# A two-layer hybrid attention block: sinks added by token, ones rows by DMA, output weights split over two steps, tail items spread over half tiles

## The chip, the cores and the metric

The kernel runs on one core of a Trainium2 chip. Its time is the device time of one execution in microseconds (us). Before the change three runs gave 1835.01 us as the median (1831.78 to 1839.63). Engines are named as the profile names them: PE (TensorE, matrix products), DVE (VectorE), ACT (ScalarE), POOL (GpSimd) and SP, which here only issues DMAs. Each engine works through its instructions in the order in which the program gives them, and waits at each for what it needs.

## The reference

Two layers (DEPTH = 2) over 1280 tokens, 256 of context and 1024 latent, at width 1024. A layer is

```
h   = adaLN-modulated RMSNorm(x)
p   = h @ w_in                                 # columns of four head groups, each with a SiLU gate
A   = multi-head latent attention, 4 heads
B   = global attention, 4 heads on 2 key heads
C   = window attention (|q - k| <= 128) + context keys, 4 heads, a sink in each softmax
D   = Mamba-2 scan, both directions
x   = x + gate * (concat(A, B, C, D) @ w_out)
```

Context tokens read only context tokens. The window heads have a sink, one learned number per head that joins each token's softmax as one more column and is then dropped, so it only adds to the softmax's denominator:

```
sink_col = jnp.broadcast_to(sink.astype(jnp.float32).reshape(kvh, g)[None, None, :, :, None, None], s_ctx.shape[:-1] + (1,))
p = jax.nn.softmax(jnp.concatenate([s_ctx, s_loc, sink_col], axis=-1), axis=-1).astype(v.dtype)
out = einsum(p over context keys, v_ctx) + einsum(p over window keys, v_band)      # the sink's column has no value
```

The second layer computes no context rows after its keys and values, and a last RMSNorm follows it.

## The kernel before

**Stages.** For each layer in turn: norm, `in_proj`, `attention`, `out_proj`. A float32 product is made of three products of rounded halves (L127 to L130: hi by hi, hi by lo, lo by hi), so each weight is fetched (`_raw`), cast to `_hi` and subtracted to `_lo`.

**Units of attention.** The pairs of heads come in the order (1,0), (1,1) for B, (0,0), (0,1) for A, (2,0), (2,1) for C. The tokens form `GROUPS = [(0,256), (256,512), (768,512)]`; a pair goes through them in the order 1, 2, 0 in the first layer and 1, 2 in the second. One (pair, group) is a unit, `main` at L1199. It goes over key blocks of 128. In each, PE makes scores (L1223, L1225, L1226), ACT takes the exponential into a tile `P` (L1227), values are multiplied in batches (L1235), and `add` sums the `P`s over the blocks: the first two in one POOL instruction (L1244, it creates `ac`), then block by block, on DVE for head 0 of every second block and on POOL else (L1250).

**The maximum.** Scores are shifted by each token's maximum, which `maxima` finds ahead, spread by `plan` over the unit before: PE `ps_s` (L1143, L1145) into a ring of three PSUM tiles, DVE reductions `mp` (L1147), at the end `mt` (L1166; for C also L1169, the maximum with the sink). Then `row` transposes `mt` (L1173), ACT negates it to `ng` (L1175), and SP writes `ng` into row 64 (or 96) of the second query tile `ql` (L1177). The matching row of the key tile holds ones (L1043, DVE copies), so the product L1226 subtracts the maximum.

**The sink.** After the second block of a C unit, `sink` (L1252) makes on ACT exp(sink - maximum) from that row of `ql`, one partition by up to 512 tokens, per head (L1256), and DVE adds it into partition 64 of `ac` (L1258).

**The tail.** What ends a unit runs in pieces during the next: `output` (L1282 ACT, L1283 POOL), two empty pieces, `token_sums` (PE transposes `ac` into `ps_sum` L1293, ACT sums over keys with 16 short instructions `junk` L1296, DVE reciprocal `asum` L1299), an empty piece, `finish` (PE `ps_rt` L1303, ACT `rrow` L1305, DMAs through DRAM into `rb`, DVE `y` L1313).

**Output weights.** During the units of the last pair, (2,1), up to three pieces of `w_out` each are fetched and split (`late`, L1543: SP DMA L1550, DVE cast L1557, DVE subtraction L1558, in halves of 512 columns). The landing tile `wo_raw` comes from the same ring of six tiles (`bg`) as `P`. What is then missing of the eight pieces is fetched and split at the start of `out_proj` (L286 SP, L289 ACT, L290 DVE). `out_proj` makes two halves of 24 products per token tile (L128 to L130, `ps_o`), casts and splits `y` (`yh` L1388 on ACT, `yl` L1389 on DVE), and runs every tail item that is left after its first tile (L1437).

**What sets the order.** In attention PE's order is written out by hand (`order_of_pe`); the other engines' order is made by the framework's scheduler.

Of the kernel before, what the change touches and what calls it, by code (L numbers as in the profile page):

```python
# [17 lines left out]
P = 128  # L18
# [39 lines left out]
def hybrid_block(ctx, tc, x, ctxt, c_t, w_fm, w_tm, w_mod, b_gate, p_col, p_row, w_qu, w_kvu, w_out,  # L58
# [125 lines left out]
    d_rms = [dp.tile([NTILE, P], F32, name=f"d_rms{i}") for i in range(3)]  # L184
    n_rms = [0]
    d_x = dp.tile([NT, DM], F32, name="d_x")

    pcol, prow, modt = {}, {}, {}

# [846 lines left out]
    def attention(L, res, need_ctx, y, late, ahead):  # L1036
# [2 lines left out]
        groups = GROUPS if need_ctx else GROUPS[1:]  # L1039

        def ones_row(tok, row):
            for lo, n in ((0, NCTX), (NCTX, NLAT)):
                nc.vector.tensor_copy(tok(lo, n, row, row + 1), ones[row:row + 1, 0:1].to_broadcast([1, n]))  # L1043

        def rows(tok, p0, src, with_ctx=True):

# [80 lines left out]
        def maxima(op, gi):  # L1127
            lo, n = GROUPS[gi]
            nt = n // P
            br, kd = op["br"], op["kd"]  # L1130
            km = kd if br == 0 else P
            npc = 1 if gi == 0 else (3 if br < 2 else 2)
            st = {}

            def scored(h, parts, dst):

                qh = op["q"][h][0]
                kh = op["k"][h][0] if br == 0 else op["k"][0][0]
                p = ps("MX", name="ps_s")
                w = parts[0][2]  # L1140
                for u, (t, k0, w, mo) in enumerate(parts):
                    o = p[:, u * w:(u + 1) * w]
                    mm(o, lhsT=qh(lo + t * P, P, 0, km), rhs=kh(k0, w, 0, km), start=True, stop=mo is None)  # L1143
                    if mo is not None:
                        mm(o, lhsT=ident_r, rhs=mask_r[:, mo:mo + w], start=False, stop=True)  # L1145
                nu = len(parts)
                nc.vector.tensor_reduce(out=dst, in_=p[:, :nu * w].rearrange("p (u k) -> p u k", u=nu), axis=AX.X, op=ALU.max)  # L1147

            def begin():
                st["mp"] = small([P, 2, 4, 3], "mp", "mp", 2)  # L1150

            def ctx_part(h, t2):
                scored(h, [(t2 + u, 0, NCTX, None) for u in range(2)], st["mp"][:, h, t2:t2 + 2, 0])

            def lat_part(h, t, c):
                if br < 2:
                    scored(h, [(t, NCTX + c * 512, 512, None)], st["mp"][:, h, t, 1 + c:2 + c])
                else:
                    i = lo // P + t
                    j0, j1 = max(2, i - 1), min(NTILE - 1, i + 1)  # L1160
                    scored(h, [(t, j0 * P, (j1 - j0 + 1) * P, (j0 - i + 1) * P)], st["mp"][:, h, t, 1:2])

            def end():
                mt = st["mt"] = small([P, 8], "mt", "mt", 2)
                mv = mt[:, 0:2 * nt].rearrange("p (h t) -> p h t", h=2)
                nc.vector.tensor_reduce(out=mv, in_=st["mp"][:, :, 0:nt, 0:npc], axis=AX.X, op=ALU.max)  # L1166
                if br == 2:
                    p0 = op["pair"] * 2
                    nc.vector.tensor_tensor(out=mv, in0=mv, in1=sink8[:, p0:p0 + 2].unsqueeze(2).to_broadcast([P, 2, nt]), op=ALU.max)  # L1169

            def row():
                pm = ps("TR", name="ps_m")
                nc.tensor.transpose(pm[0:2 * nt, 0:P], st["mt"][:, :2 * nt], ident)  # L1173
                ng = tm((8, P), F32R, name="ng")
                nc.scalar.activation(out=ng[0:2 * nt, :], in_=pm[0:2 * nt, 0:P], func=AF.Copy, scale=-1.0)  # L1175
                for h in range(2):
                    nc.sync.dma_start(out=f32(op["q"][h][1](lo, n, kd, kd + 1)), in_=f32(ng[h * nt:(h + 1) * nt, :]))  # L1177

            r = [begin]
            for h in range(2):  # L1180
                r += [lambda h=h, t=t: ctx_part(h, t) for t in range(0, nt, 2)]
                if gi > 0:
                    r += [lambda h=h, t=t, c=c: lat_part(h, t, c) for t in range(nt) for c in range(2 if br < 2 else 1)]
            return r + [end], row
# [14 lines left out]
        def main(op, gi, steps, tail):  # L1199
# [38 lines left out]
            def add(bi, pts):  # L1238
# [7 lines left out]
                else:  # L1246
                    s = sums[0]
                    for h in range(2):
                        eng = nc.vector if h == 0 and bi % 2 == 0 else nc.gpsimd
                        eng.tensor_tensor(out=s[:, h, c0:c0 + w], in0=s[:, h, c0:c0 + w], in1=pts[:, h, :w], op=ALU.add)  # L1250

            def sink():  # L1252
                for h in range(2):
                    hd = op["pair"] * 2 + h
                    es = tm(name="es")
                    nc.scalar.activation(out=es[64:65, :n], in_=f32(op["q"][h][1](lo, n, 64, 65)), func=AF.Exp,  # L1256
                                         scale=HEAD_SCALE, bias=pr[64:65, PR_SINK + hd:PR_SINK + hd + 1])
                    nc.vector.tensor_tensor(out=sums[0][64:65, h, :n], in0=sums[0][64:65, h, :n], in1=es[64:65, :n], op=ALU.add)  # L1258

            nb = -(-len(blocks) // BATCH)  # L1260
            ends = [-(-len(blocks) * (b + 1) // nb) - 1 for b in range(nb)]
# [28 lines left out]
            def token_sums(h):  # L1290
                pss = ps("TR", name="ps_sum")
                for t in range(nt):
                    nc.tensor.transpose(pss[:, t * P:(t + 1) * P], sums[0][:, h, t * P:(t + 1) * P], ident)  # L1293
                for t in range(nt):
                    junk = tm((P, P), name="junk")
                    nc.scalar.activation(out=junk, in_=pss[:, t * P:(t + 1) * P], func=AF.Copy, scale=2.0,  # L1296
                                         accum_out=ss[:, h * nt + t:h * nt + t + 1])
                if h == 1:
                    nc.vector.reciprocal(out=ss[:, :2 * nt], in_=ss[:, :2 * nt])  # L1299

            def finish():
# [9 lines left out]
                    nc.sync.dma_start(out=rb[h * 64:h * 64 + 64, :n],  # L1311
                                      in_=dr[h * nt:(h + 1) * nt, :].rearrange("t q -> (t q)").unsqueeze(0).to_broadcast([64, n]))
                nc.vector.tensor_tensor(out=y[br * 2 + op["pair"]](lo, n), in0=rb[:, :n], in1=o[:, :n], op=ALU.mult)  # L1313
            idle = lambda: None
            return tail + [output, idle, idle, lambda: [token_sums(h) for h in range(2)], idle, finish]

        def plan(blocks, pieces, row, loose):

# [23 lines left out]
            return r + more, row  # L1342

        first, row = prep(*pairs[0])
        yield first + [row]
        y_slots, tail = [], []
        order_of_pe = ExitStack()
        order_of_pe.enter_context(tc.manual_schedule(engines={mybir.EngineType.PE}))
        for i, (br, pair) in enumerate(pairs):
            op = ops[br, pair]  # L1350
            if need_ctx and i == 0:
                pk = Slot([P, 4, NCTX], F32, "y_cx")
                y_slots.append(pk)
            if need_ctx and br == 2:
                pk = res["ssd"].y_slots[0]
            s = Slot([P, NLAT], F32, f"y{br}{pair}")
            y_slots.append(s)
            y[br * 2 + pair] = Tok(pk.t[:, br * 2 + pair - (2 if br == 2 else 0), :] if need_ctx else None, s.t)
            for gi in gorder:
                pieces, row, loose = [], None, []  # L1360
                if gi == 1:
                    pieces, row = maxima(op, 2)
                    if need_ctx:
                        loose, late_row = maxima(op, 0)
                elif gi == 2:
                    if i + 1 < len(pairs):
                        pieces, row = prep(*pairs[i + 1])
                if i + 1 == len(pairs):
                    loose = loose + sum((late() for _ in range(N_LATE)), [])
                if i + 1 == len(pairs) and gi == 0:  # L1370
                    ahead()
                steps = plan(len(key_blocks(br, gi)), pieces, row, loose)
                if gi == 2 and need_ctx:
                    steps[4][0].append(late_row)
                tail = main(op, gi, steps, tail)
        order_of_pe.close()
        while len(tail) > 5:
            tail.pop(0)()
        if not need_ctx:
            ahead()  # L1380
        yield y_slots, tail
# [10 lines left out]
    def out_proj(L, y, need_ctx, wo, tail, y_slots, pairs):  # L1392
# [27 lines left out]
        for t in ts:  # L1420
# [5 lines left out]
            for j in range(2):  # L1426
# [7 lines left out]
                if j == 0:  # L1434
                    ssq = small([P, 2], "ssq", "ssq", 4)
                half_ssq(xt.t, j, ssq)
            if t == ts[0]:  # L1437
                for f in tail:
                    f()
            if not last:  # L1440
                if t >= 2:
                    nc.sync.dma_start(out=d_x[c, :], in_=xt.t)
# [73 lines left out]
    for L in range(DEPTH):  # L1516
# [23 lines left out]
        def ahead():  # L1540
            y_pairs[2] = y_pair(y, 2)

        def late():  # L1543

            st = []

            def first():
                if len(wo) < 8 and len(free_slots) >= 2:
                    raw = bg(name="wo_raw")
                    nc.sync.dma_start(out=raw, in_=w_out[L, len(wo)])  # L1550
                    st.extend([raw, Slot([P, 1024], F32R, "wo_hi"), Slot([P, 1024], F32R, "wo_lo")])
                    wo.append(st[1:])

            def half(j):
                if st:
                    js = slice(j * 512, (j + 1) * 512)
                    nc.vector.tensor_copy(st[1].t[:, js], st[0][:, js])  # L1557
                    nc.vector.tensor_tensor(out=st[2].t[:, js], in0=st[0][:, js], in1=f32(st[1].t[:, js]), op=ALU.subtract)  # L1558
            return [first, lambda: None, lambda: half(0), lambda: half(1)]
# [95 lines left out]
```

## Time and profile before

| | us |
|---|---|
| median of three runs | 1835.01 |
| profiled execution | 1834.35 |
| its span | 1832.6 |
| PE busy | 1724.8 (94%) |
| DVE busy | 1159.6 (63%) |
| POOL busy | 777.4 (42%) |
| ACT busy | 747.1 (41%) |

The mean granted clock of PE over the span is 0.982 of full speed. Window attention (pairs of C) is at 790 to 870 us in the first layer and 1655 to 1732 in the second, each followed by its `out_proj`. A row of a timeline gives start, duration, engine, line, operation, out<-in, shape and, in brackets, how long the engine was idle before it and what ended the wait. Consecutive like instructions are put in one row with their count (x2). L12 is line 12 of the kernel before.

### The profile page before, as it was taken

Reading aid. Unit: us, or ns where it says so; the run is one execution under the profiler, and the core shown is the slowest. Engines: PE = TensorE matmul, PEld = TensorE weight load, DVE = VectorE, ACT = ScalarE, POOL = GpSimd, SP = SyncE. Lnnn points to the kernel's source line nnn. Section 1 sums busy time; section 2 is a strip of 40 time slices with the busy share of each in tenths; the row PEclk is TensorE's granted clock in tenths of the full one; section 3 lists DMA queues with packets and bytes.
Section 4 is the critical chain, followed back from the end, with each engine's and each line's share of the span. In section 5 each row is a group of like instructions: output and inputs, shape, how many; then the busy total and the mean of one; then the engine's idle time right before and its main releaser. Section 6 shows DMA issues by size and latency. Waiting matters only on the chain. (4 is left out here: it accounts for less than half of the span.)

```text
span 1832.6 us, 27875 instructions
## 1 busy us (share of the span) xinstructions
PE 1724.8 (94%) x9658; PEld 1340.1 (73%) x9658; DVE 1159.6 (63%) x2290; ACT 747.1 (41%) x2060; POOL 777.4 (42%) x735
## 2 busy tenths in 40 slices
PE   6999999999989999998999989999998999999898
PEld 4667888889975566665787768888997656667576
DVE  6867864374468766557646777753743887655753
ACT  5433433332225545455423323343322355456531
POOL 2322552132317766655324224531332477665422
PEclk9999999999999999998999989999999999999899
DMA  9474323255576232223411524231668633220511
GB/s 314 143 235 142 125 90 121 82 195 178 187 209 151 71 102 65 70 62 111 172 58 41 170 85 150 83 126 70 209 187 240 180 86 88 73 54 20 180 72 58
DMA packets 130396, 231.52 MB, mean 126 GB/s; under 512 B 13784, under 2 KB 74560, under 8 KB 130256
## 3 DMA queue, kind: packets, MB, share of 16 engines
q1 hardware_dynamic: 130256, 229.75, 40.1%
q8 instruction: 76, 1.25, 0.3%
q14 instruction: 64, 0.52, 0.1%
HBM read 161.15 MB, written 68.44 MB: 125 GB/s over the span
## 5 line engine op out<-in xcount | busy, mean ns | idle before, releaser
L1250 POOL TENSOR_TENSOR ac<-ac,P 128x512 f32<-128x512 f32 (+3 forms) x248 | 305.3, 1249 | 153.1 <-ACT P L1227 99.8
L1227 ACT ACTIVATE P<-ps_st 128x512 f32<-128x512 f32 (+3 forms) x456 | 243.2, 552 | 239.1 <-PE ps_st L1226 104.4
L1147 DVE TENSOR_REDUCE mp<-ps_s 128x1 f32<-128x512 f32 (+3 forms) x428 | 259.7, 657 | 102.0 <-PE ps_s L1143 96.3
L128 PE MATMUL ps_fm<-hh,wfm_hi 128*128 128x512 f32 x576 | 234.6, 407 | 3.3 <-DVE kb L658 1.9
L130 PE MATMUL ps_fm<-hl,wfm_hi 128*128 128x512 f32 x576 | 232.1, 403 | 1.5 <-POOL hl L403 0.7
L129 PE MATMUL ps_fm<-hh,wfm_lo 128*128 128x512 f32 x576 | 230.7, 400 | 0.0
L128 PE MATMUL ps_tm<-wtm_hi,hh 128*128 128x256 f32 x512 | 146.6, 286 | 2.0 <-DVE qkv L723 1.3
L129 PE MATMUL ps_tm<-wtm_hi,hl 128*128 128x256 f32 x512 | 145.6, 284 | 0.0
L130 PE MATMUL ps_tm<-wtm_lo,hh 128*128 128x256 f32 x512 | 145.4, 284 | 0.0
L1250 DVE TENSOR_TENSOR ac<-ac,P 128x512 f32<-128x512 f32 (+3 forms) x88 | 102.5, 1165 | 49.4 <-ACT P L1227 25.7
L130 PEld LDWEIGHTS ps_fm<-hl,wfm_hi 128*128 128x128 f32 x576 | 109.6, 190 | 27.1 <-POOL hl L403 3.2
L128 PEld LDWEIGHTS ps_fm<-hh,wfm_hi 128*128 128x128 f32 x576 | 109.9, 191 | 26.6 <-ACT hf L399 3.3
L129 PEld LDWEIGHTS ps_fm<-hh,wfm_lo 128*128 128x128 f32 x576 | 109.8, 191 | 19.4 <-issue 0.8
L1244 POOL TENSOR_TENSOR ac<-P 128x1024 f32<-128x1024 f32 (+1 forms) x30 | 66.1, 2205 | 116.2 <-ACT P L1227 103.0
L128 PE MATMUL ps_o<-wo_hi,yh 128*128 128x512 f32 x288 | 112.8, 393 | 1.4 <-ACT yh L1388 1.4
L129 PE MATMUL ps_o<-wo_hi,yl 128*128 128x512 f32 x288 | 112.8, 393 | 0.1
L130 PE MATMUL ps_o<-wo_lo,yh 128*128 128x512 f32 x288 | 112.7, 392 | 0.0
L128 PEld LDWEIGHTS ps_tm<-wtm_hi,hh 128*128 128x128 f32 x512 | 98.2, 192 | 4.3 <-issue 3.4
L130 PEld LDWEIGHTS ps_tm<-wtm_lo,hh 128*128 128x128 f32 x512 | 98.3, 192 | 0.7 <-issue 0.4
L129 PEld LDWEIGHTS ps_tm<-wtm_hi,hl 128*128 128x128 f32 x512 | 98.2, 192 | 0.5
L1235 PE MATMUL ps_acc<-P,vt 128*64 128x512 f32 (+3 forms) x416 | 84.5, 536 | 4.1 <-ACT P L1227 4.1
L1223 PE MATMUL ps_st<-qq,kk 128*128 128x512 f32 (+3 forms) x208 | 82.4, 396 | 2.9 <-DVE mp L1147 2.7
(345 smaller groups left out, 4125.0 us busy)
## 6 DMA issues: line engine op xcount, KB each, us to landing
wfm_raw<-in_w_fm_dram SPq DMA_DIRECT2D x36, 512.0 KB
wm<-in_w_mod_dram SPq DMA_DIRECT2D x64, 256.0 KB
d_q<-qkhl SPq DMA_DIRECT2D x18, 512.0 KB
wm<-in_w_mod_dram SPq DMA_DIRECT2D x16, 512.0 KB
d_gate<-th SPq DMA_DIRECT2D x32, 256.0 KB
wtm_raw<-in_w_tm_dram SPq DMA_DIRECT2D x16, 512.0 KB
qq<-d_q SPq DMA_DIRECT2D x32, 256.0 KB
wo_raw<-in_w_out_dram SPq DMA_DIRECT2D x16, 512.0 KB
```

The source lines that it names most:

```text
L128: mm(o, lhsT=lh, rhs=rh, start=first, stop=False)
L129: mm(o, lhsT=ll, rhs=rh, start=False, stop=False)
L130: return mm(o, lhsT=lh, rhs=rl, start=False, stop=last)
L1147: nc.vector.tensor_reduce(out=dst, in_=p[:, :nu * w].rearrange("p (u k) -> p u k", u=nu), axis=AX.X, op=ALU.max)
L1223: mm(st, lhsT=k(k0, 128), rhs=q(q0, 128), start=True, stop=False)
L1227: nc.scalar.activation(out=pts[:, h, :w], in_=st, func=AF.Exp, scale=op["scale"])
L1235: mm(acc[h * 64:h * 64 + 64, c0:c0 + w], lhsT=op["v"].tile(kb)[:, v0:v0 + 64], rhs=pts[:, h, :w], start=(bi == 0), stop=(bi == len(blocks) ...
L1244: nc.gpsimd.tensor_tensor(out=s[:, :, :n], in0=sums[0][:, :, :n], in1=pts[:, :, :n], op=ALU.add)
L1250: eng.tensor_tensor(out=s[:, h, c0:c0 + w], in0=s[:, h, c0:c0 + w], in1=pts[:, h, :w], op=ALU.add)
```

## The change

Five edits. (1) The ones rows of key tiles are written by DMA from a DRAM row `d_one`, which one DMA makes at the start; DVE's 32 copies go, SP gets 32 issues more. (2) The sinks are added where a token's sums stand: `end` makes the negated maximum `mr` on DVE (in all 30 units), a C unit adds the sink to it (128x8), takes the exponential on ACT (128x8) and adds it into `asum` before the reciprocal. The 20 instructions of L1256 on ACT and the 20 of L1258 on DVE go. (3) `late` may also run for the pair before the last, in groups 2 and 0, two pieces each, if three slots are free. (4) Empty tail items are dropped before `out_proj`, and one tail item runs per half tile. (5) Four empty pieces are put behind the first unit's `row`.

```diff
+    d_one = dp.tile([1, NT], F32, name="d_one")
+    nc.sync.dma_start(out=d_one.rearrange("o (a b) -> o a b", b=P), in_=ones[0:1, :].unsqueeze(1).to_broadcast([1, NTILE, P]))
...
         def ones_row(tok, row):
-            for lo, n in ((0, NCTX), (NCTX, NLAT)):
-                nc.vector.tensor_copy(tok(lo, n, row, row + 1), ones[row:row + 1, 0:1].to_broadcast([1, n]))
+            rows(tok, row, d_one)
...
             def end():
-                mt = st["mt"] = small([P, 8], "mt", "mt", 2)
+                mt = small([P, 8], "mt", "mt", 2)
...
+                st["mr"] = op["mr", gi] = small([P, 8], "mr", "mr", 4, F32R)
+                nc.vector.tensor_scalar(out=st["mr"][:, :2 * nt], in0=mt[:, :2 * nt], scalar1=-1.0, scalar2=None, op0=ALU.mult)
...
-                nc.scalar.activation(out=ng[0:2 * nt, :], in_=pm[0:2 * nt, 0:P], func=AF.Copy, scale=-1.0)
+                nc.scalar.copy(ng[0:2 * nt, :], pm[0:2 * nt, 0:P])
...
+            es = [None]
+
             def sink():
-                for h in range(2):
-                    hd = op["pair"] * 2 + h
-                    es = tm(name="es")
-                    nc.scalar.activation(out=es[64:65, :n], in_=f32(op["q"][h][1](lo, n, 64, 65)), func=AF.Exp,
-                                         scale=HEAD_SCALE, bias=pr[64:65, PR_SINK + hd:PR_SINK + hd + 1])
-                    nc.vector.tensor_tensor(out=sums[0][64:65, h, :n], in0=sums[0][64:65, h, :n], in1=es[64:65, :n], op=ALU.add)
+
+                es[0] = small([P, 8], "es", "es", 3)
+                v = es[0][:, :2 * nt].rearrange("p (h t) -> p h t", h=2)
+                p0 = op["pair"] * 2
+                nc.vector.tensor_tensor(out=v, in0=f32(op["mr", gi][:, :2 * nt]).rearrange("p (h t) -> p h t", h=2),
+                                        in1=sink8[:, p0:p0 + 2].unsqueeze(2).to_broadcast([P, 2, nt]), op=ALU.add)
+                nc.scalar.activation(out=es[0][:, :2 * nt], in_=es[0][:, :2 * nt], func=AF.Exp, scale=HEAD_SCALE)
...
+                if h == 1 and br == 2:
+                    nc.vector.scalar_tensor_tensor(out=ss[:, :2 * nt], in0=es[0][:, :2 * nt], scalar=2.0, in1=ss[:, :2 * nt],
+                                                   op0=ALU.mult, op1=ALU.add)
...
-        yield first + [row]
+        yield first + [row] + [idle] * 4
...
-                    loose = loose + sum((late() for _ in range(N_LATE)), [])
+                    loose = loose + sum((late(0) for _ in range(N_LATE)), [])
+                elif i + 2 == len(pairs) and gi != 1:
+                    loose = loose + sum((late(1) for _ in range(2)), [])
...
+        tail = [f for f in tail if f is not idle]
...
-            if t == ts[0]:
-                for f in tail:
-                    f()
+                if tail:
+                    tail.pop(0)()
...
-                if len(wo) < 8 and len(free_slots) >= 2:
+                if len(wo) < 8 and len(free_slots) >= 2 + keep:
```

PE has the same number of instructions before and after. Of the eight pieces of `w_out`, `out_proj` itself fetches one in the first layer before and after, and two in the second layer before, none after. In the first layer three pieces now come in pair (2,0), in the second layer two.

DVE's order is shown first at the second layer, from the maxima of unit (2,1) group 1 on (tiles `mp_17276` before, `mp_17335` after), which are made during unit (2,0) group 2 and beside unit (2,1) group 1. Before:

```order
1895 L1147 TENSOR_REDUCE mp_17276<-ps_s_17304 128x1
1896 L1147 TENSOR_REDUCE mp_17276<-ps_s_17312 128x1
1897 L1313 TENSOR_TENSOR y20_16837<-rb_17244,o_17040 128x512
1898 L1147 TENSOR_REDUCE mp_17276<-ps_s_17330 128x2
1899 L1258 TENSOR_TENSOR ac_17316<-ac_17316,es_17318 1x512
1900 L1258 TENSOR_TENSOR ac_17316<-ac_17316,es_17321 1x512
1901 L1147 TENSOR_REDUCE mp_17276<-ps_s_17334 128x2
1902 L1147 TENSOR_REDUCE mp_17276<-ps_s_17343 128x1
```

The same stretch after the change, with the second piece of `w_out` that is moved into pair (2,0):

```order
1891 L1254 TENSOR_TENSOR ac_17150<-ac_17150,P_17303 128x256
1892 L1148 TENSOR_REDUCE mp_17335<-ps_s_17336 128x2
1893 L1148 TENSOR_REDUCE mp_17335<-ps_s_17344 128x2
1894 L1571 CAST wo_hi_17290<-wo_raw_17288 128x512 x2
1895 L1572 TENSOR_TENSOR wo_lo_17291<-wo_raw_17288,wo_hi_17290 128x512 x2
1896 L1148 TENSOR_REDUCE mp_17335<-ps_s_17348 128x1
1897 L1148 TENSOR_REDUCE mp_17335<-ps_s_17359 128x1
1898 L1148 TENSOR_REDUCE mp_17335<-ps_s_17363 128x1
1899 L1148 TENSOR_REDUCE mp_17335<-ps_s_17371 128x1
1900 L1323 TENSOR_TENSOR y20_16881<-rb_17299,o_17083 128x512
1901 L1148 TENSOR_REDUCE mp_17335<-ps_s_17386 128x2
1902 L1148 TENSOR_REDUCE mp_17335<-ps_s_17390 128x2
```

The two additions of the sink into `ac` no longer stand between reductions, and a split of one piece stands between the second and the third reduction.

ACT's order is shown in the first layer in unit (2,1) group 2, where `P_9104` before is `P_9150` after. Before:

```order
766 L1227 ACTIVATE P_9087<-ps_st_9088 128x128
767 L1227 ACTIVATE P_9087<-ps_st_9097 128x128
768 L1227 ACTIVATE P_9104<-ps_st_9105 128x256
769 L1282 COPY o_9033<-ps_acc_8780 128x512
770 L1256 ACTIVATE es_9075<-ql0_8505,con_69 1x512
771 L1256 ACTIVATE es_9078<-ql1_8506,con_69 1x512
772 L1175 ACTIVATE ng_9083<-ps_m_9081 4x128
773 L1227 ACTIVATE P_9104<-ps_st_9110 128x256
```

The same stretch after the change:

```order
763 L1265 ACTIVATE es_9296<-es_9296 128x4
764 L1231 ACTIVATE P_9137<-ps_st_9138 128x128
765 L1231 ACTIVATE P_9137<-ps_st_9143 128x128
766 L1231 ACTIVATE P_9150<-ps_st_9151 128x256
767 L1231 ACTIVATE P_9150<-ps_st_9156 128x256
768 L1289 COPY o_9086<-ps_acc_8830 128x512
769 L1179 CAST ng_9133<-ps_m_9131 4x128
```

Both halves of `P` now follow one another, and the copy of `o` and the row `ng` come behind them.

DVE's order at the end of pair (2,0) in the first layer, where group 0 of that pair runs and the maxima of (2,1) begin. Before:

```order
948 L1250 TENSOR_TENSOR ac_8576<-ac_8576,P_8682 128x384
949 L1250 TENSOR_TENSOR ac_8576<-ac_8576,P_8723 128x256
950 L1258 TENSOR_TENSOR ac_8765<-ac_8765,es_8767 1x256
951 L1258 TENSOR_TENSOR ac_8765<-ac_8765,es_8770 1x256
952 L1147 TENSOR_REDUCE mp_8786<-ps_s_8787 128x2
953 L1147 TENSOR_REDUCE mp_8786<-ps_s_8795 128x2
```

The same stretch after the change:

```order
950 L1254 TENSOR_TENSOR ac_8605<-ac_8605,P_8711 128x384
951 L1254 TENSOR_TENSOR ac_8605<-ac_8605,P_8764 128x256
952 L1571 CAST wo_hi_8719<-wo_raw_8717 128x512 x2
953 L1572 TENSOR_TENSOR wo_lo_8720<-wo_raw_8717,wo_hi_8719 128x512 x2
954 L1571 CAST wo_hi_8751<-wo_raw_8749 128x512 x2
955 L1572 TENSOR_TENSOR wo_lo_8752<-wo_raw_8749,wo_hi_8751 128x512 x2
956 L1148 TENSOR_REDUCE mp_8836<-ps_s_8837 128x2
957 L1148 TENSOR_REDUCE mp_8836<-ps_s_8845 128x2
```

Two splits of four instructions each now stand ahead of the first reduction.

## Rows read from the trace of the kernel before

**Rows 1.** The page, busy time of each engine, share of the span, instructions.
```profile
PE 1724.8 (94%) x9658; PEld 1340.1 (73%) x9658; DVE 1159.6 (63%) x2290; ACT 747.1 (41%) x2060; POOL 777.4 (42%) x735
```
**Rows 2.** Windows by stretch: us, busy time of each engine, granted clock, DMA share, GB/s.
```profile
790.00:870.00 80.00, 68.98 (x405) 49.13 (x404) 56.76 (x105) 46.66 (x170) 41.32 (x39) 0.91 0.25 77
...
1655.00:1732.00 77.00, 66.51 (x385) 50.06 (x384) 52.39 (x93) 42.68 (x146) 41.35 (x38) 0.91 0.24 77
```
**Rows 3.** Windows of 5 us behind the longer waits, same columns.
```profile
815.00:820.00 5.00, 4.88 (x20) 2.98 (x22) 2.20 (x8) 2.28 (x16) 1.41 (x2) 0.66 0.00 0
...
855.00:860.00 5.00, 2.17 (x6) 0.77 (x8) 4.94 (x9) 4.31 (x18) 2.50 (x2) 0.50 0.28 103
...
1700.00:1705.00 5.00, 5.00 (x25) 3.43 (x26) 1.74 (x6) 2.77 (x17) 1.99 (x2) 0.73 0.01 3
...
1720.00:1725.00 5.00, 4.38 (x14) 3.62 (x15) 4.74 (x10) 3.18 (x16) 1.51 (x2) 0.50 0.88 302
1725.00:1730.00 5.00, 4.68 (x17) 2.78 (x17) 4.59 (x6) 3.37 (x12) 4.34 (x5) 0.50 0.46 141
...
1755.00:1760.00 5.00, 5.00 (x18) 3.98 (x18) 1.10 (x2) 2.12 (x9) 1.27 (x1) 0.77 0.18 52
```
**Rows 4.** Timeline of PE, window attention of the first layer: products that waited.
```profile
797.19 1.94 PE L1235 MATMUL ps_acc<-P,pk 128*64 128x512 f32 x8 [1.47 <-DVE mp L1147]
...
815.12 0.62 PE L1143 MATMUL ps_s<-kk,qq 128*128 128x384 f32 x1 [2.79 <-DVE mp L1147]
...
853.37 1.33 PE L1293 MATMUL ps_sum<-con,ac 128*128 128x128 f32 x5 [2.18 <-DVE ac L1250]
857.83 3.68 PE L1235 MATMUL ps_acc<-P,pk 128*64 128x512 f32 x8 [3.13 <-ACT ng L1175]
```
**Rows 5.** Timeline of DVE and of ACT around those waits.
```profile
811.32 2.36 DVE L1258 TENSOR_TENSOR ac<-ac,es 1x512 f32<-1x512 f32 x2 [0.28 <-POOL ac L1244]
...
856.16 1.32 ACT L1256 ACTIVATE es<-ql,con 1x512 f32<-1x512 f32 x2
```
**Rows 6.** Timeline of PE, window attention and out_proj of the second layer.
```profile
1679.73 0.39 PE L1223 MATMUL ps_st<-qq,kk 128*128 128x256 f32 x1 [2.73 <-DVE mp L1147]
...
1699.07 0.53 PE L1143 MATMUL ps_s<-kk,qq 128*128 128x384 f32 x1 [3.37 <-DVE mp L1147]
...
1720.62 1.39 PE L1235 MATMUL ps_acc<-P,vt 128*64 128x256 f32 x4 [4.07 <-ACT P L1227]
...
1740.69 0.73 PE L128 MATMUL ps_o<-wo_hi,yh 128*128 128x512 f32 x2 [1.40 <-ACT yh L1388]
...
1752.87 0.27 PE L1303 MATMUL ps_rt<-con,asum 128*8 128x128 f32 x1 [2.12 <-DVE asum L1299]
```
**Rows 7.** Timeline of DVE in the same stretch.
```profile
1677.80 1.29 DVE L1258 TENSOR_TENSOR ac<-ac,es 1x512 f32<-1x512 f32 x2 [2.27 <-POOL ac L1244]
1679.12 2.08 DVE L1147 TENSOR_REDUCE mp<-ps_s 128x1 f32<-128x384 f32 x4
...
1713.04 4.03 DVE L1557 CAST wo_hi<-wo_raw 128x512 fp32r<-128x512 f32 x2 [0.97 <-DMA wo_raw<-in_w_out_dram]
1717.00 1.28 DVE L1558 TENSOR_TENSOR wo_lo<-wo_raw,wo_hi 128x512 fp32r<-128x512 f32 x2
```
**Rows 8.** Waits of PE, 787 to 900: us in total, times, longest.
```profile
PE ps_rt L1303 <- DVE asum L1299: 2.3, 3, 1.0
```
**Rows 9.** Tiles: duration ns min/median/max, first and last start us, forms.
```profile
L1258 DVE TENSOR_TENSOR ac<-ac,es x20: 409/676/1757, 794.8 to 1722.7; 1x512 f32<-1x512 f32 x16, 1x256 f32<-1x256 f32 x4
...
L1557 DVE CAST wo_hi<-wo_raw x26: 395/413/2621, 846.4 to 1732.5; 128x512 fp32r<-128x512 f32 x26
...
L1169 DVE TENSOR_TENSOR mt<-mt,con x10: 163/168/1065, 774.9 to 1701.4; 128x8 f32<-128x8 f32 x8, 128x4 f32<-128x4 f32 x2
...
L1177 SPq DMA_DIRECT2D ql<-ng x48: 572/627/715, 543.4 to 1708.5; - x48
```
**Rows 10.** Source L1043: who waited for the line: us, times.
```profile
  PEld ps_st L1218: 1.6, 2
```

More of the change, by code (lines that the diff above doesn't have):

```diff
@@ L1169, in end @@
                     nc.vector.tensor_tensor(out=mv, in0=mv, in1=sink8[:, p0:p0 + 2].unsqueeze(2).to_broadcast([P, 2, nt]), op=ALU.max)
+                st["mr"] = op["mr", gi] = small([P, 8], "mr", "mr", 4, F32R)
+                nc.vector.tensor_scalar(out=st["mr"][:, :2 * nt], in0=mt[:, :2 * nt], scalar1=-1.0, scalar2=None, op0=ALU.mult)
             def row():
                 pm = ps("TR", name="ps_m")
-                nc.tensor.transpose(pm[0:2 * nt, 0:P], st["mt"][:, :2 * nt], ident)
+                nc.tensor.transpose(pm[0:2 * nt, 0:P], f32(st["mr"][:, :2 * nt]), ident)
                 ng = tm((8, P), F32R, name="ng")
-                nc.scalar.activation(out=ng[0:2 * nt, :], in_=pm[0:2 * nt, 0:P], func=AF.Copy, scale=-1.0)
+                nc.scalar.copy(ng[0:2 * nt, :], pm[0:2 * nt, 0:P])
                 for h in range(2):
@@ L1313, in finish, with idle @@
                 nc.vector.tensor_tensor(out=y[br * 2 + op["pair"]](lo, n), in0=rb[:, :n], in1=o[:, :n], op=ALU.mult)
-            idle = lambda: None
             return tail + [output, idle, idle, lambda: [token_sums(h) for h in range(2)], idle, finish]
+        def idle():
+            pass
         def plan(blocks, pieces, row, loose):
@@ L1541, in ahead, with late @@
             y_pairs[2] = y_pair(y, 2)
-        def late():
+        def late(keep):
             st = []
             def first():
-                if len(wo) < 8 and len(free_slots) >= 2:
+                if len(wo) < 8 and len(free_slots) >= 2 + keep:
                     raw = bg(name="wo_raw")
```

## The prediction

> **What bounds the kernel now.** I read the busy times first, then the windows by stretch, then PE's timeline inside the stretches that fall short, and last the timelines of the engines that PE's rows name. The busy times show PE at 94% of the span, far above DVE with 63% [rows 1]. So a gain can only come from PE's idle time and from its slow clock. The windows show where these are: in window attention PE works 68.98 of 80 us at a granted clock of 0.91 in the first layer and 66.51 of 77 us at 0.91 in the second [rows 2], 21.5 us idle together, while over the whole span the idle part is 6%. The timeline of PE then names single waits. In the first layer they are 1.47, 2.79, 2.18 and 3.13 us [rows 4]; in the second 2.73, 3.37 and 4.07, and after them in out_proj 1.40 and 2.12 [rows 6]; first-layer out_proj adds 2.3 us in three waits for `asum` [rows 8]. Behind the longer ones PE's clock is low for a while, 0.66, 0.50, 0.73, 0.50 twice and 0.77 [rows 3]: a granted clock of 0.50 is the 1.2 GHz level, and in each case PE had just been idle for over 2 us. The change touches just these places, so I go through them one by one.
>
> **The sink's additions.** Two DVE instructions per C unit, twenty in all, go, with a median of 0.676 us each [rows 9]. What matters is that they wait for POOL's first sum, and that the maxima stand behind them in DVE's order (the first two order pieces show them between two reductions). At 811.32 DVE waited 0.28 us and then worked 2.36 us [rows 5]; PE waited 2.79 us for the reduction behind [rows 4]. After the change, reductions that are ready run in that time, so I take this wait at 815.12 away whole: 2.8 us. The wait of 1.47 us at 797.19 is of the same kind: 1.5 us. The slow window behind 815.12 had 4.88 us of busy PE at 0.66, which is (1 - 0.66) x 4.88 = 1.7 us that comes back. In the second layer DVE waited 2.27 us and worked 1.29 [rows 7], and PE waited 2.73 us [rows 6]; four reductions of 2.08 us in all [rows 7] fit into the freed 3.56 us: 2.7 us.
>
> The wait of 3.37 us at 1699.07 [rows 6] is less clear, since the change puts a split of `w_out` between the second and third reduction of the same unit (first pair of order pieces). A split is two casts, 0.41 us each alone [rows 9], and two subtractions, 1.28 us together [rows 7]: 2.1 us. DVE stays late there, only earlier in the unit; I take 0.8 us of the 3.37. Behind it 5.00 us ran at 0.73 [rows 3], 1.35 us lost, and with a shorter wait I take half back, 0.7.
>
> What is added per C unit are three DVE operations on 128x8 and one ACT exponential. The nearest row is the 128x8 maximum with the sink, 0.168 us [rows 9], so 0.5 us against 1.35 us that go, off PE's path. The new `mr` stands in the path from the last maximum to the row in `ql` in all 30 units; in 28 of them other products lie between, and only in the first unit of each layer the product that needs the row stands right behind the transposition in PE's order, so it costs 2 x 0.17 = 0.3 us. If that cover failed in all, it would be 30 x 0.17 = 5 us; if the earlier reductions hide it, nothing.
>
> **ACT's order in the first layer.** The 3.13 us at 857.83 [rows 4] come from ACT: between the two halves of one `P` stood the copy of `o`, two exponentials of the sink of 1.32 us together [rows 5], and `ng`. The second pair of order pieces shows the two halves together now. The first half itself had waited for a ring tile, which a piece of `w_out` held; that wait may stay in part. I take 2.5 us, with 1.3 and 3.1 as ends. The wait before it, 2.18 us on DVE's sum at 853.37, is one DVE addition beside POOL's first sum, and nothing in the change touches it. Since it stays, of the 2.17 us of products at 0.50 [rows 3], 1.1 us lost, I take half back, 0.5.
>
> The sum for the first layer's window attention is 2.8 + 1.5 + 1.7 + 2.5 + 0.5 = 9.0 us, and for the second's 2.7 + 0.8 + 0.7 = 4.2 us. The largest single wait there, 4.07 us at 1720.62 with 2.2 and 2.3 us of slow clock behind it [rows 3, 6], stays: `P` waits for a ring tile that the third piece of `w_out` in that unit holds, and the number of pieces in (2,1) in this layer is the same after the change.
>
> **out_proj.** In the second layer the two pieces that out_proj split itself are gone, and with them the 1.40 us in which `yh` came late [rows 6]: 1.4 us. The 2.12 us at 1752.87 [rows 6] are the 16 short ACT sums, which stood behind the second half's sum of squares. After the change they come half a tile, 24 products, sooner and the product that needs them stands behind 12 products of the next tile; I take 1.6 of the 2.12 us away, and of the slow 5.00 us at 0.77 [rows 3], 1.15 us lost, 1.0. In the first layer I take 1.2 of the 2.3 us of waits for `asum` [rows 8], half, because 14 subtractions of `yl` now stand ahead of that reciprocal on DVE. Sum: 1.4 + 1.6 + 1.0 + 1.2 = 5.2 us. Should the sums stay late, only the 1.4 us are left; should all go, it is 7.0 us (5.8 of waits, 1.15 of clock).
>
> **The moved splits.** Five pieces come into pair (2,0), where no piece was split before, three in the first layer and two in the second. The first two are shown in the last order pieces, ahead of the first maxima of (2,1). DVE is busy 56.76 of 80 us in that stretch [rows 2], so 5 x 2.1 us fit into its idle time as such; what can cost is that DVE waits for the landing piece with reductions queued behind it, and that the piece holds a ring tile of `P`. From below it is nothing. From above it is what the 13 pieces of before (26 half casts [rows 9]) cost: the waits at 857.83 and 1720.62 had a piece in their chain, 7.2 us, or 0.55 each. I take the upper value, 5 x 0.55 = 2.8 us lost, since pair (2,0) now has what (2,1) had.
>
> **Ones rows, row ahead, empty pieces.** PE's weight loads waited 1.6 us in two places for the copies of L1043 [rows 10]. The DMAs that replace them are in the same stretch of SP's queue as the other rows of the same tiles, each issue as the 0.627 us of `ng` [rows 9]; 32 of them are 20 us of SP over two layers, and what is queued behind are other rows that are fetched a unit ahead. I cost both at nothing: the 1.6 us may come back, or a key tile may come as late by one DMA. The four empty pieces bring the first `row` forward in the plan only; PE's order has the transposition behind the same product as before. Nothing.
>
> **The sum.** 9.0 + 4.2 + 5.2 - 0.3 - 2.8 = 15.3 us off the profiled execution's 1834.35 us gives 1819.0. That execution is 0.7 us below the median of the three runs, so the forecast is 1820 us. If every touched wait (19.3 us: 1.47, 2.79, 3.13, 2.73, 3.37, 2.3, 1.40, 2.12) and the clock behind them (1.7 + 1.1 + 1.35 + 1.15 = 5.3 us) came back, and the 1.6 us of L1043, it would be 26.2 us and 1809; that is the low end, less a little for what is not listed: 1808.
>
> **Rival 1: POOL's first sum still holds DVE.** DVE's next block sum (L1250) needs the same `ac` and stands in DVE's order too. If the maxima still wait behind it, the sink terms fall out: 2.8 + 1.5 + 1.7 + 2.7 + 0.8 + 0.7 = 10.2 us of the 15.3, and the time is 1830. For it speaks that at 1677.80 DVE waited 2.27 us for POOL and not for ACT [rows 7]. Against it speaks the order: after the change the reductions of that stretch stand ahead of the next block sum, 2.08 us of work for four [rows 7], nearly as long as that wait.
>
> **Rival 2, slower: the moved splits repeat the stall of 1720.** There a pair of casts took 4.03 us [rows 7] where two alone take 0.8 [rows 9], the piece kept its ring tile so much longer, ACT could not write the next `P`, and PE lost 4.07 us [rows 6] and 4.5 us of clock, (1 - 0.50) x (4.38 + 4.68) [rows 3]: 8.6 us. The same can happen in the three steps of (2,0) that now have pieces, 25.8 us. Without my 2.8 us for them the gain is 18.1, so the time is 1834.35 + 25.8 - 18.1 + 0.7 = 1843. It decides from two of the three steps on (17.2 us). For it speaks that in (2,0) DVE meets POOL's first sums as in (2,1); against it that (2,0) has at most two pieces a step instead of three, that three free slots are asked for, and that 11 of the 13 pieces of before stand in no long wait.
>
> What the casts waited for in that row has a rule in the Trainium skill, SBUF — State Buffer, section "SBUF: two separate sides": VectorE and GpSimd share a pair of ports, held by one of them for a whole instruction while the other is blocked, where the VectorE instruction is of a two-port kind or has two SBUF inputs. By this rule the 4.03 us and the 2.621 us maximum of the casts [rows 9] agree with a hold by POOL, every moved piece that meets a POOL sum would be held by 4.03 - 0.8 = 3.2 us, and five of them by 16 us of DVE time, which would make the time 1833 if PE paid all of it. The trace bears it out only for some pieces, as the median of 0.413 us shows.
>
> **Chances.** The forecast's case 0.65, with a range of its own of 1812 to 1827; rival 1 0.22; rival 2 0.13. A measurement of this kernel can tell some 0.5%, 9.2 us, from no change, so faster means below 1825.8 and slower above 1844.2. Of the forecast's case 0.59 lies below 1825.8, of rival 1 0.04: faster 0.63. Rival 2 lies at the upper bound, 0.07 of it above: slower 0.07. The rest is 0.30. The range of 1808 to 1840 leaves out about 0.04 below and 0.10 above.
>
> **What would show it.** In the profile after, window attention should fall to about 71 and 73 us, PE should wait at no `ps_s` or `ps_st` for `mp` by over 1 us in the first layer, the wait behind 1720 should still be there with its clock of 0.50, and out_proj of the second layer should show no wait of over 1 us in its first two tiles. Splits of `w_out` in pair (2,0) should take about 2 us each on DVE. The prediction is wrong if casts of 2 us or more stand in (2,0) with ACT waiting behind them, if DVE waits for POOL's first sum with reductions queued, or if SP's added rows make PE wait for `ql` or a key tile anywhere in the pairs of A and B.

## The result and the profile after

The changed kernel takes 1820.89 us (median of six runs, 1815.12 to 1822.48) against 1836.48 us of the kernel before beside it; the ratio is 0.9911 (95% interval 0.9892 to 0.9930). A second measurement gave 1816.40 us, ratio 0.9883 (0.9861 to 0.9905). The forecast was 1820. The profiled execution, 1815.12 us, is the fastest of its six. Lines of the kernel have moved by some ten: L1043's copies are gone, 1148 is `mp`, 1231 `P`, 1239 `ps_acc`, 1248 POOL's first sum, 1254 the later ones, 1309 `asum`, 1313 `ps_rt`, 1571 and 1572 the late split.

The page's first part answers [rows 1]: DVE has 18 us less to do, and PE 6 with the same number of instructions, at a mean granted clock of 0.985 instead of 0.982.

```profile
PE 1718.6 (95%) x9658; PEld 1340.2 (74%) x9658; DVE 1141.4 (63%) x2294; ACT 734.4 (40%) x2048; POOL 785.7 (43%) x735
```

Windows of the two stretches of window attention, as in [rows 2] but each 74 us here, and below them the 5 us behind the two longest new waits:

```profile
790.00:864.00 74.00, 65.71 (x412) 48.82 (x410) 57.59 (x113) 41.50 (x170) 42.50 (x37) 0.95 0.30 93
1641.00:1715.00 74.00, 64.58 (x380) 48.27 (x376) 60.49 (x97) 37.32 (x141) 44.05 (x38) 0.95 0.28 93
...
834.00:839.00 5.00, 5.00 (x27) 4.74 (x27) 3.72 (x9) 1.78 (x5) 0.92 (x2) 0.71 0.36 65
1683.00:1688.00 5.00, 4.79 (x22) 4.75 (x23) 5.00 (x12) 1.12 (x3) 1.31 (x2) 0.66 0.33 107
```

The stretches are 6 and 3 us shorter, and the granted clock is 0.95 instead of 0.91, but 17.7 us of them are still idle. Rows of PE's timeline, with others between them left out, show which waits went and which came:

```profile
796.16 1.94 PE L1239 MATMUL ps_acc<-P,pk 128*64 128x512 f32 x8
811.30 0.34 PE L1144 MATMUL ps_s<-kk,qq 128*128 128x384 f32 x1
827.43 0.44 PE L1144 MATMUL ps_s<-kk,qq 128*128 128x384 f32 x1 [1.13 <-DVE mp L1148]
833.86 0.37 PE L1313 MATMUL ps_rt<-con,asum 128*8 128x128 f32 x1 [4.51 <-DVE asum L1309]
849.51 0.27 PE L1313 MATMUL ps_rt<-con,asum 128*4 128x128 f32 x1 [1.33 <-DVE asum L1309]
852.06 1.04 PE L1300 MATMUL ps_sum<-con,ac 128*128 128x128 f32 x8
853.17 1.94 PE L1239 MATMUL ps_acc<-P,pk 128*64 128x512 f32 x8
...
1664.44 0.39 PE L1227 MATMUL ps_st<-qq,kk 128*128 128x256 f32 x1 [0.87 <-DVE mp L1148]
1683.21 0.47 PE L1227 MATMUL ps_st<-qq,kk 128*128 128x256 f32 x1 [2.69 <-DVE mp L1148]
1706.33 0.92 PE L1239 MATMUL ps_acc<-P,vt 128*64 128x256 f32 x4 [4.10 <-ACT P L1231]
1715.82 0.50 PE L129 MATMUL ps_o<-wo_hi,yl 128*128 128x512 f32 x1 [1.59 <-DVE yl L1404]
1731.90 0.27 PE L1313 MATMUL ps_rt<-con,asum 128*8 128x128 f32 x1 [0.69 <-ACT yh L1403]
```

All four waits of [rows 4] are gone at their places: the rows at 796.16, 811.30, 852.06 and 853.17 have no bracket, where 1.47, 2.79, 2.18 and 3.13 us stood. The 4.07 us of [rows 6] are still there, 4.10, as forecast. New are 1.13 us for `mp` and 4.51 and 1.33 us for `asum` in the first layer, and 2.69 us for `mp` in the second. The waits of 1.13, 4.51 and 2.69 us stand in the first unit of pair (2,1), which begins at 822.68 and 1674.28 us: pieces of `w_out` that were moved into pair (2,0) are in part split only there. So the reductions in the first order pieces of the section on the change are those for unit (2,1) group 2, made during unit (2,1) group 1. The 1.33 us are not theirs: with the sinks added by token and no piece moved, the same product waits 1.34 us.

DVE's timeline ahead of the end of the 4.51 us:

```profile
828.37 0.74 DVE L1571 CAST wo_hi<-wo_raw 128x512 fp32r<-128x512 f32 x2
829.03 1.28 DVE L1572 TENSOR_TENSOR wo_lo<-wo_raw,wo_hi 128x512 fp32r<-128x512 f32 x2
830.24 2.82 DVE L1323 TENSOR_TENSOR y<-rb,o 128x512 f32<-128x512 f32 x1
832.98 0.15 DVE L1306 SCALAR_TENSOR_TENSOR asum<-es,asum 128x8 f32<-128x8 f32 x1
833.06 0.55 DVE L1148 TENSOR_REDUCE mp<-ps_s 128x1 f32<-128x384 f32 x1
833.52 0.19 DVE L1309 RECIPROCAL asum<-asum 128x8 f32<-128x8 f32 x1
```

and DVE and POOL ahead of the end of the 2.69 us, with POOL's sum beside the `y` above as the first row:

```profile
829.87 2.64 POOL L1248 TENSOR_TENSOR ac<-P 128x1024 f32<-128x1024 f32 x1 [3.64 <-issue]
...
1678.18 4.51 DVE L1572 TENSOR_TENSOR wo_lo<-wo_raw,wo_hi 128x512 fp32r<-128x512 f32 x2
1678.09 1.29 POOL L1290 TENSOR_TENSOR o<-o,gate 128x512 f32<-128x512 f32 x1 [1.98 <-ACT o L1289]
1679.35 2.79 POOL L1248 TENSOR_TENSOR ac<-P 128x1024 f32<-128x1024 f32 x1
```

A split delays DVE twice: by its own 2.0 us, and by pushing what follows into POOL's first sum. `y` took 2.82 us there, against a median of 0.69 us, and the two subtractions 4.51 us (1.75 and 2.84) against 1.28. The reciprocal that PE needs in the first layer, and the reductions in the second, stand behind all of it. The Trainium skill, SBUF — State Buffer, section "SBUF: two separate sides", has a rule for this: a VectorE instruction with two SBUF inputs and a GpSimd instruction that reads SBUF share a port pair that one of them holds for a whole instruction. The trace agrees: the two subtractions and `y` each begin behind a POOL instruction and each end 0.55 us behind its end (`y` at 833.06, POOL's sum at 832.51 us).

An estimate of what the moved pieces cost PE, from these rows: 4.51 us less the 0.72 that the product waits without them (shown below), 1.13 and 2.69 us of waiting, and behind them 5.00 us at 0.71 and 4.79 us at 0.66, 1.5 and 1.6 us lost, some 11 us in all.

### The profile page after: what moved, and what is told of

Read it like the earlier page. It is cut to its first block, busy times and chain, and to the rows that moved or that the text cites. A ratio compares the mean times of both kernels' runs of the same rounds, so it can differ in the third digit from the quotient of the medians.

```text
span 1813.3 us, 27884 instructions
## 1 busy us (share of the span) xinstructions
PE 1718.6 (95%) x9658; PEld 1340.2 (74%) x9658; DVE 1141.4 (63%) x2294; ACT 734.4 (40%) x2048; POOL 785.7 (43%) x735
## 4 chain that ended last, share of the span: by engine, by line
PE 71%; DVE 13%; DMA 5%; POOL 4%; issue 4%; ACT 2%; SPq 1%; POOLq 0%; DVEq 0%; ACTq 0%
PE ps_acc L1239 9%; PE ps_fm L128 7%; PE ps_fm L130 7%; PE ps_fm L129 7%; PE ps_s L1144 5%; PE ps_o L130 3%; PE ps_o L129 3%; PE ps_o L128 3%; PE ps_st L1227 3%; PE ps_st L1230 2%; PE ps_st L1222 2%; PE ps_st L1224 2%; PE ps_st L1223 2%; PE ps_tm L128 2%; PE ps_tm L129 2%
## 5 line engine op out<-in xcount | busy, mean ns | idle before, releaser
L1254 DVE TENSOR_TENSOR ac<-ac,P 128x512 f32<-128x512 f32 (+3 forms) x88 | 96.2, 1094 | 48.7 <-ACT P L1231 23.7
L1248 POOL TENSOR_TENSOR ac<-P 128x1024 f32<-128x1024 f32 (+1 forms) x30 | 69.8, 2325 | 112.2 <-ACT P L1231 92.6
```

Of the source, the lines that this page charges most:

```text
L1248: nc.gpsimd.tensor_tensor(out=s[:, :, :n], in0=sums[0][:, :, :n], in1=pts[:, :, :n], op=ALU.add)
```

## The experiments

Each kernel ran with the kernel before beside it; ratios are against that one, with 95% intervals. Four make one edit on the kernel before; the others take edits out of the changed kernel, or ask what in it costs.

**Sinks by token alone.** On the kernel before, `end`, `row`, `sink` and the line in `token_sums` as in the change, nothing else.

> The kernel before with edit 2 alone (sinks added by token, negated maximum on DVE). Theory A: most of the gain is here, 13 us as the prediction sums it for both stretches of window attention: 1823 us, ratio 0.993, and PE shows no wait of over 1.5 us for mp in window attention. Rival 1 of the prediction (POOL's first sum still holds DVE): 5 us or less, 1831 us or more, ratio 0.997. Theory D: without the splits in pair (2,0) the sinks' part is larger than in the whole change, since the wait of 3.4 us and its slow clock in the second layer go too: 1819 us, ratio 0.990.

Measured 1821.07 us, 0.9907 (0.9893 to 0.9921): 16 to 17 us, more than A and near D. Rival 1 is out. PE's waits in window attention of the second layer:

```profile
PE ps_acc L1238 <- ACT P L1230: 4.1, 1, 4.1
PE ps_rt L1312 <- DVE asum L1308: 1.0, 1, 1.0
PE ps_st L1226 <- DVE mp L1147: 0.9, 1, 0.9
```

The 3.37 us of [rows 6] are gone whole here; in the changed kernel the moved split keeps 2.69 of them. But in the first layer, in unit (2,1) group 2, a wait came that the kernel before does not have, for a reciprocal behind DVE's splits there:

```profile
856.79 0.37 PE L1312 MATMUL ps_rt<-con,asum 128*8 128x128 f32 x1 [4.28 <-DVE asum L1308]
```

**Ones rows by DMA alone.**

```diff
-            for lo, n in ((0, NCTX), (NCTX, NLAT)):
-                nc.vector.tensor_copy(tok(lo, n, row, row + 1), ones[row:row + 1, 0:1].to_broadcast([1, n]))
+            rows(tok, row, d_one)
```

> The kernel before with edit 1 alone: ones rows by DMA. Theory A (from the run without edit 1, 6 us slower than the whole change): DVE's copies hold reductions, above all the four at 595 to 602 us with PE's wait of 2.4 us for mp at 603 us behind them; that wait and its slow clock go, 1829 to 1831 us, ratio 0.997. Theory B (the prediction): nothing, 1836 us, ratio 1.000. Theory C: the ones rows gain only where the sinks are gone too, since DVE has other waits else: 1835 us, and the wait at 603 us goes all the same.

Measured 1828.17 us, 0.9955 (0.9938 to 0.9972): 8 us. Theory B, the prediction, is out. The trace of the kernel before has the cause in a stretch that the prediction passed over (DVE, and below it PE):

```profile
595.45 1.25 DVE L1043 CAST kh_cx<-con 1x256 fp32r<-1x256 f32 x1
596.62 1.76 DVE L1043 CAST kh<-con 1x1024 fp32r<-1x1024 f32 x1
598.31 1.36 DVE L1043 CAST kh_cx<-con 1x256 fp32r<-1x256 f32 x1
600.87 1.74 DVE L1043 CAST kh<-con 1x1024 fp32r<-1x1024 f32 x1 [1.20 <-POOL o L1283]
602.64 1.89 DVE L1147 TENSOR_REDUCE mp<-ps_s 128x2 f32<-128x512 f32 x3
...
603.48 0.99 PE L1293 MATMUL ps_sum<-con,ac 128*128 128x128 f32 x4 [2.42 <-DVE mp L1147]
```

Four copies of one partition, 6.1 us, one of which waited 1.20 us more, by the trace for POOL, kept the reductions back. With DMAs the same products run without a wait:

```profile
603.37 1.04 PE L1294 MATMUL ps_sum<-con,ac 128*128 128x128 f32 x8
```

The granted clock in the 5 us from 603 us on is 0.66 before and 1.00 with DMAs. Product by product against the kernel before (the two profiled executions are 6.5 us apart), some 4 us come in that place, under 1 us at 678 us (`mp` again), 1.6 us behind 815 us and some 4 us in the second layer's in_proj. Some 3 us are lost ahead of them, in the first layer's in_proj, where a wait of 4.95 us for `rb` takes the place of one of 3.26 us for `qkv`. The 1.6 us are the clock alone: PE waits 2.83 us there, as the 2.79 us before, but the 5 us from 813.5 us on ran at 1.00 and not at 0.66 [rows 3]. Why in_proj gains and loses I did not follow, nor steps of under 1 us. So the copies ahead of `mp` are shown as the cause of some 5 us; how the rest adds up to 8 is not shown.

**Moved splits alone.** On the kernel before, `late(keep)` and the two lines for the pair before the last.

> The kernel before with edit 3 alone. Theory A: the moved splits cost the same 15 us beside the old sinks: 1850 us, ratio 1.008. Theory B: here DVE waits for POOL's first sum anyway, and the splits run partly in those waits: 1840 us, ratio 1.002. The prediction's price (2.8 us lost, 1.4 us back in out_proj): 1838 us, ratio 1.001.

Measured 1838.69 us, 1.0013 (1.0001 to 1.0026): 2 to 3 us slower, the prediction's price. In the first layer PE waits here for `P`:

```profile
834.06 0.69 PE L1143 MATMUL ps_s<-kk,qq 128*128 128x384 f32 x1 [4.39 <-ACT P L1227]
```

By the trace ACT had lost 1.77 us waiting for DVE's addition of a sink, which stood behind two splits. The 3.13 us of [rows 4] are gone here, and 3.62 us stand in place of the 3.37 us of [rows 6].

**Tail items alone.** On the kernel before, idle items dropped and one item per half tile.

> The kernel before with edit 4 alone: empty tail items dropped, one tail item per half tile. Theory A (the prediction's terms for it, 1.6 + 1.0 + 1.2): 1832 us, ratio 0.998, and the wait of 2.1 us for asum in the second out_proj is gone. Theory B (the two runs without edit 3 differ by 2.4 us): 1833 us. Theory C (the run without edit 4 was 5 us faster than the whole change): it costs, 1838 us or more.

Measured 1834.12 us, 0.9986 (0.9970 to 1.0002): 2.6 us, which the interval does not tell from nothing. C is out; A and B cannot be told apart. The wait of 2.12 us for `asum` is gone, and 1.80 us for `yh` stand where 1.40 did.

**The change without the moved splits.**

```diff
-                    loose = loose + sum((late(0) for _ in range(N_LATE)), [])
-                elif i + 2 == len(pairs) and gi != 1:
-                    loose = loose + sum((late(1) for _ in range(2)), [])
+                    loose = loose + sum((late() for _ in range(N_LATE)), [])
...
-                if len(wo) < 8 and len(free_slots) >= 2 + keep:
+                if len(wo) < 8 and len(free_slots) >= 2:
```

> The changed kernel without edit 3: no piece of the output weights is split in pair (2,0), two pieces are split in the second out_proj again. Theory A (from the trace of the changed kernel): the moved splits cost PE about 9 us in pair (2,0) (4.5 us waiting for asum and 1.3 us in the first layer, 2.7 us waiting for mp in the second, with slow clock behind), and give back 1.4 us in the second out_proj, so the time falls to 1812 to 1815 us, ratio to the kernel before 0.987. Theory B: the moved splits pay for themselves, since they relieve pair (2,1) and out_proj; then the time rises to 1824 us or more, ratio 0.993. Theory C (the prediction's price of 2.8 us for them, less the 1.4 us that come back): 1819 to 1820 us, ratio 0.991.

Measured 1805.83 us, 0.9833 (0.9814 to 0.9852): 9 to 14 us faster than the change (by its second and first ratio), more than A. The 4.51 us wait is 0.72, and the 1.13 and 2.69 us are gone:

```profile
826.65 0.27 PE L1313 MATMUL ps_rt<-con,asum 128*8 128x128 f32 x1 [0.72 <-DVE asum L1309]
```

**The change with the moved pieces, but without DVE's part of them.** The five pieces come by two DMAs each and hold other numbers than the weights; their landing tile, casts and subtractions are left out.

```diff
-                if len(wo) < 8 and len(free_slots) >= 2 + keep:
+                if keep and len(wo) < 8 and len(free_slots) >= 2 + keep:
+                    both = Slot([P, 1024], F32R, "wo_hi"), Slot([P, 1024], F32R, "wo_lo")
+                    for b in both:
+                        nc.sync.dma_start(out=f32(b.t), in_=d_q[0][:, 0, 0, 0:1024])
+                    wo.append(both)
+                elif len(wo) < 8 and len(free_slots) >= 2 + keep:
```

> The whole change, but the five pieces that edit 3 moves into pair (2,0) are written to wo_hi and wo_lo by two DMAs each, from another DRAM tensor, without a landing tile of the ring and without DVE's cast and subtraction; these five pieces hold other numbers than the output weights. Theory A: the 15 us that edit 3 costs are DVE's time ahead of reciprocals and reductions, so they go: 1806 to 1809 us, ratio 0.984. Theory B: the cost lies in the fetches on the queue and in the memory traffic, which are doubled here: 1820 us or more, ratio 0.991.

Measured 1809.35 us, 0.9848 (0.9829 to 0.9867). Most of the cost goes with DVE's work and the ring tile, and twice the transfers cost little: A, not B. PE's waits for `asum` in the first layer fall from 7.1 us in all to

```profile
PE ps_rt L1313 <- DVE asum L1309: 2.3, 3, 1.3
```

and in the second layer PE waits no longer than 0.9 us for `mp` or `P` ahead of the wait for `P` in the last unit, which is 4.20 us here. Two waits came in the first layer's (2,0), 1.34 us for `P` and 1.20 us for `mp`. DVE's time and the ring tile are not parted by this run; in the trace of the change it is DVE that PE waits for.

**The change without edits 3 and 4.**

> The changed kernel without edits 3 and 4: sinks by token, ones rows by DMA, nothing moved in the tail. Compared with the run without edit 3 (1805.8 us, ratio 0.983) it shows what the tail edit is worth where no split stands in pair (2,0). Theory A (the prediction): the tail edit gains 2.6 to 4 us, so this run takes 1808 to 1810 us, ratio 0.985. Theory B (the run without edit 4 was 5 us faster than the whole change): the tail edit costs, and this run takes 1800 to 1802 us, ratio 0.981. Theory C: neither, 1806 us.

Measured 1808.50 us, 0.9846 (0.9827 to 0.9865): the time that A gave and not B's. The tail edit would be worth some 2 us again, but the intervals of this run and of the one without edit 3 overlap, so C, nothing, is not out.

**The change without edit 4, twice, and the change again beside the second.**

> The changed kernel without edit 4: all tail items run after out_proj's first tile again, empty ones included. Theory A: the edit is worth the 1.6 us of the wait for the ACT sums, 1.0 us of clock and part of the 1.2 us in the first layer: 1824 us, ratio 0.993, and a wait of about 2 us for asum stands in the second out_proj again. Rival: the wait was hidden otherwise once the output weights are there earlier, 1821 us, ratio 0.991, no wait.

> The changed kernel without edit 4 once more, beside the run before it. Theory A: ratio 0.988, 5 us faster than the whole change, so that the tail edit costs where splits stand in pair (2,0). Theory B: ratio as that of the whole change within 0.001.

> The changed kernel once more, on the chip of the next run. Theory A: the 5 us between it and the run without edit 4 are real: ratio 0.991 here and 0.988 there, and out_proj shows where. Theory B: they are the spread between calls: both ratios within 0.001 of each other, near 0.989.

Without edit 4 it is 0.9884 (0.9870 to 0.9898) and 0.9894 (0.9870 to 0.9918); the change beside the second is 0.9883. So the 5 us between the first runs were spread between measurements, and with splits in (2,0) the tail edit changes nothing that can be measured, though PE waits 0.69 us where it waits 1.40 us without the edit and [rows 6] has 2.12.

**The change without edit 1.**

> The changed kernel without edit 1: DVE copies the ones rows again. Theory A (prediction): nothing, 1821 us, ratio 0.991. Rival: DVE's 25 us of copies stand ahead of reductions at the start of attention and in the pairs of B, where the trace of the changed kernel has lost a wait of 2.4 us of PE for mp at 603 us and its slow clock: 1825 to 1827 us, ratio 0.994, with that wait back.

Measured 1827.08 us, 0.9942 (0.9927 to 0.9957): 6 to 11 us slower than the change, the rival. The wait is back:

```profile
611.82 0.63 PE L1299 MATMUL ps_sum<-con,ac 128*128 128x128 f32 x4 [2.43 <-DVE mp L1147]
```

**Without the moved splits, and late casts on ACT.** In `half`, `nc.vector.tensor_copy` becomes `nc.scalar.copy`.

> The changed kernel without edit 3, and with the casts of the late pieces (13 in pair (2,1) over both layers) on ACT. Theory A: the splits in (2,1) hold PE by way of DVE, as in (2,0): the wait for asum at 855 us (2.2 us) and the one for P in the second layer (4.1 us, where two casts took 4.0 us beside POOL) get shorter, 1801 to 1803 us, ratio 0.981. Theory B: ACT is what makes P late in (2,1), and 26 casts of about 0.5 us ahead of exponentials cost PE as much: 1806 us or more, ratio 0.984.

Measured 1804.21 us, 0.9823 (0.9806 to 0.9841), not to be told from the run without edit 3, and between A and B. The 4.3 us for `P` and 2.2 us for `asum` are gone, but PE now waits for ACT's copy of `o`, behind casts, and in the first layer also behind a `P` for which ACT waited 1.40 us by the trace for DVE's subtraction:

```profile
PE ps_acc L1239 <- ACT o L1289: 3.2, 1, 3.2
...
PE ps_st L1227 <- ACT o L1289: 2.6, 1, 2.6
```

The first row is of the first layer, the second of the second layer. The three versions without the moved splits beat both kernels.

## Why the prediction was right

The time was right, and half of its reasons; two terms were wrong by about the same amount with opposite signs, so that the time came out so near is luck. Several of the signs that the prediction named did not come: window attention is 74 and 74 us long, not 71 and 73; in the first layer PE waits 1.13 us for `mp`; in out_proj it waits 1.59 us for `yl`; and of the five moved splits only one takes 2 us on DVE, the others 2.5, 4.1, 4.4 and 5.2. One of its signs of being wrong did come in another form: DVE is held beside POOL's first sum with reductions queued, by the subtractions.

- **Sinks, window attention: 12.9 us (13.2 less 0.3 for `mr`).** Right in mechanism and nearly in size: 16 to 17 alone. The waits named went, and the 2.18 us at 853 us, which was to stay, went too, in this run and in the change: it was one DVE sum at 850.89 us that took 2.42 us beside POOL's first sum (from 850.33), and takes 0.28 us in the change, where POOL starts at 851.44. Not foreseen was the new wait for a reciprocal in (2,1) group 2, 4.28 us in this run and 1.05 in the change: DVE came to it late, behind splits, a product of the tail and the sinks' addition.
- **Ones rows: nothing.** This term failed. "I cost both at nothing", from the 1.6 us that PE's weight loads waited [rows 10]. That row lists only who waited for the copies themselves. What they cost is in instructions queued behind them on DVE, here `mp`, and a wait put down to `mp` does not name them. Measured: 8 us alone, of which some 5 are traced to them, 6 to 11 in the change.
- **Moved splits: 2.8 us lost, 1.4 back.** The price is right on the kernel before, 2 to 3 us net. In the change they cost 9 to 14. In the kernel before, long waits stood in pair (2,1) already, and the splits mostly moved them: the 3.37 us went, and 3.62 us came a few products earlier in the unit; the 3.13 us went, and 4.39 us came in the unit before. With the sinks gone, the split is what comes last. So the term was mis-sized, most likely because it was priced by a trace with the old waits in it. The mechanism of rival 2 was half right: POOL did hold the splits, but in the change PE waited for `asum` and `mp` behind them, not for `P`; on the kernel before it did wait for `P`.
- **out_proj: 5.2 us.** The 1.40 us for `yh` and the 2.12 us for `asum` went, but 1.59 us for `yl` came. The 2.3 us of [rows 8] include 0.20 us ahead of out_proj; the two waits in the first layer's out_proj, 1.05 and 1.02 us, did not shrink but became 1.34 and 1.20. The tail edit measures 2.6 us alone, not clear of noise, and nothing in the change.
- **The 4.07 us in the second layer stays:** right, 4.10 us.
- **Row ahead, empty pieces: nothing.** The first product that needs `ql` waits 2.14 us for it after the change, at 550 us, and 2.17 us before it. No run had this edit alone.

Alone, the four edits that were run sum to 17 + 8 + 3 - 2 = 26 us; together they give 16 to 21. The difference is the moved splits, which cost more once the others are in: without them the rest give 31 us, and 17 + 8 + 3 = 28 alone.

## What to carry to other kernels

A wait is listed under the instruction that released it; before an edit that takes work off an engine that runs in order is priced at nothing, read what is queued behind that work and who waits for that. When two edits touch one engine, price each on the trace that the other leaves: a wait that hides a new cost may be what the other edit removes. And run a bundle's edits apart: here the bundle without one edit is 0.5% to 0.8% faster.

## What was not expected of the hardware

A DVE copy into a single partition is not small: 1x1024 took 0.68 to 1.78 us and 1x256 0.28 to 1.37, against 0.41 us for a cast of 128x512. The four copies shown above ran beside POOL's work. The same rows by DMA take 0.23 to 0.44 us of SP's time each. And what the clock costs behind a wait is no fixed price: behind the same wait of 2.8 us the next 5 us ran at 0.66 in the kernel before and at 1.00 with the ones rows alone.
